# Trace of batched matrix products: six unread products per row in TensorE's last row loop

## The chip, the cores and the metric

The kernel runs on one NeuronCore of a Trainium2 chip. The metric is the time of one execution on the device in microseconds (us). A core has five engines that run their own instruction streams and meet at semaphores: TensorE (PE in the profile; its weight loads are PEld), VectorE (DVE), ScalarE (ACT), GpSimd (POOL) and SyncE (SP). Each engine has a sequencer, which carries out waits, register arithmetic and branches and hands the rest to the engine. TensorE reads two operands from the on-chip memory and writes products to PSUM. Transfers from the chip's main memory run on 16 DMA engines.

## The reference

For 8 pairs of square matrices of 2176 x 2176 in float32, the result is the trace of each product:

```python
B, N = 8, 2176

def reference(a, b):
    prod = np.matmul(a, b)
    traces = np.diagonal(prod, axis1=1, axis2=2).sum(axis=-1)
    return traces.astype(np.float32)
```

The trace of a product needs no product: it is the sum over all i and k of a[i, k] times b[k, i]. So the work is to read both matrices once (8 x 2 x 18.9 MB), transpose one, multiply element by element and add up.

## The kernel before, in words

A batch is handled in pieces of 128 partitions. A matrix has 17 strips of 128 rows; a partition holds 17 rows of 2176 elements in bfloat16 (the transfers convert). `at` holds the transposed first matrix, `rows_b` the second one (and, before that, part of the first), `a_six` the rest of the first.

For each batch TensorE transposes the first matrix block by block into three PSUM slots (`slots`, lines 345 and 348), ScalarE (line 237) and VectorE (line 266) copy the slots into `at`, and VectorE multiplies `at` by `rows_b` and reduces in one instruction (`multiply_reduce`, line 249). GpSimd issues nearly all transfers (line 169), SyncE turns landings into counts for TensorE.

The last batch is treated differently. Its second matrix arrives in ten pieces (`pieces`): rows 0 to 4, 5 to 8, 9 and 10, 11 and 12, then rows 13, 14 and 15 alone, then the last row (16) in three pieces: a long one (columns 768 to 2175), columns 256 to 767, and columns 0 to 255. Each has a semaphore in `d_late`. The seven pieces of whole rows are `whole`. VectorE takes columns 0 to 1663 of each row (`SHARE` is 1664) and of the last row columns 768 to 1663. TensorE takes the rest: the last four blocks of 128 columns of each row (`ON_TENSOR` is 4), and of the last row also columns 0 to 767. It multiplies a block of `at` by the same block of `rows_b` and adds it onto one 128 x 128 tile, `trace_ps`, whose diagonal holds the wanted sums.

TensorE's part of this is the body named "close". It runs after the transposes of the last batch:

1. It waits until the PSUM slot of the last transposes is free, and makes a matmul of a zero tile (line 309) that starts the accumulation.
2. A loop over rows 0 to 15 (line 311, `first` is a register that holds the row's first column). Each turn waits on `landed` and lowers it by one (line 312), then makes four products whose addresses are worked out from `first` (line 315). SyncE raises `landed` by a piece's number of rows when the piece is there (lines 192 to 194).
3. For the three pieces of the last row it waits on the piece's own semaphore and makes four, four and two products with fixed addresses (line 321). The last one signals `added`.

VectorE then takes the diagonal of `trace_ps` into `sums`, TensorE adds over the partitions (line 353), VectorE reduces to eight numbers (line 296) and SyncE stores them (line 357).

VectorE's own loop over the pieces of the last batch covers the pieces of whole rows and the long piece of the last row.

Of the kernel before, what the change touches and what calls it, by code (L numbers as in the profile page):

```python
# [22 lines left out]
def kernel(  # L23
# [6 lines left out]
    nc = tc.nc  # L30
    P = 128
    BATCH, N, N2 = a.shape
    assert N == N2 and N % P == 0
    NT = N // P
# [7 lines left out]
    f32 = mybir.dt.float32  # L42
    MUL, ADD = mybir.AluOpType.mult, mybir.AluOpType.add
    SLOTS = 3
    ON_TENSOR, TAKEN, CLOSE = 4, 4, 4
    SHARE = N - ON_TENSOR * P

    def sbuf(name, shape, dtype):
        return nc.alloc_sbuf_tensor(name, shape, dtype).ap()

    def psum(name, shape):
        return nc.alloc_psum_tensor(name, shape, f32).ap()

    at = sbuf("at", [P, NT, N], bf16)
    a_six = sbuf("a_six", [P, TWICE, N], bf16)
    rows_b = sbuf("rows_b", [P, NT, N], bf16)
    five, b_six = rows_b[:, 0:FIVE, :], rows_b[:, FIVE:, :]
    identity32 = sbuf("identity32", [P, P], f32)
    identity16 = sbuf("identity16", [P, P], bf16)
# [5 lines left out]
    slots = [psum(f"aT{k}", [P, 8, P]) for k in range(SLOTS)]  # L65
# [50 lines left out]
    def flat(t):  # L116
        return t.rearrange("p r k -> p (r k)")
# [10 lines left out]
    class Piece:  # L128
# [9 lines left out]
    END = NT - 1  # L138
    pieces = [
        Piece(0, 5), Piece(5, 9), Piece(9, 11), Piece(11, 13), Piece(13, 14), Piece(14, 15),  # L140
        Piece(15, 16), Piece(END, NT, 6 * P, N), Piece(END, NT, 2 * P, 6 * P), Piece(END, NT, 0, 2 * P),
    ]
    whole = [piece for piece in pieces if piece.v1 < NT]

    def counted(name):
        return Counted(nc, name)
# [18 lines left out]
    gp, act, sp, dve, pe = nc.gpsimd, nc.scalar, nc.sync, nc.vector, nc.tensor  # L165
# [16 lines left out]
    for n in range(BATCH):  # L182
# [6 lines left out]
        if n == LAST:  # L189
            sp.wait_ge(d_a12.sem, 16)  # L190
        sp.sem_inc(moved)  # L191
    for k, piece in enumerate(whole):
        sp.wait_ge(d_late[k].sem, 16)
        sp.sem_inc(landed, piece.v1 - piece.v0)

# [36 lines left out]
    with nc.Fori(0, BATCH, engines=OrderedEngineSet([act.engine])):  # L232
        act.wait_ge(clear, 1).then_inc(clear, -1)  # L233
        for k, t in enumerate(on_scalar):
            _, dst, view = tiles[t]
# [12 lines left out]
    def multiply_reduce(x, y, acc, out=None):  # L248
        return dve.tensor_tensor_reduce(  # L249
            out=x if out is None else out, in0=x, in1=y, scale=1.0, scalar=0.0,  # L250
            op0=MUL, op1=ADD, accum_out=acc,
        )
# [3 lines left out]
    with nc.Fori(  # L256
        0, dve.snap(once, min_val=1, max_val=BATCH), engines=OrderedEngineSet([dve.engine]),
        hint_back_edge=True,
    ):
        for n in range(BATCH):  # L260
            for k, t in enumerate(on_vector):
                _, dst, view = tiles[t]
                if k == 0 and n:
                    dve.wait_ge(product.sem, 2 * n).then_inc(clear, 1)
                dve.wait_ge(for_vector, len(on_vector) * n + k + 1)
                ins = dve.tensor_copy(out=dst, in_=view(slots[t % SLOTS]))  # L266
                if t != on_vector[-1]:
                    ins.then_inc(free[t % SLOTS], 1)
                else:
                    vector_done.by(ins)  # L270
            dve.wait_ge(vector_done.sem, n + 1).then_inc(free[on_vector[-1] % SLOTS], 1)
            dve.wait_ge(scalar_done.sem, n + 1).then_inc(free[on_scalar[-1] % SLOTS], 1)
            if n == LAST:
                continue
            for k, (load, t, v0) in enumerate(((d_b5, five, 0), (d_b6, b_six, FIVE))):
                dve.wait_ge(load.sem, 16 * (n + 1))
                product.by(multiply_reduce(
                    flat(at[:, v0:v0 + t.shape[1], :]), flat(t), sums[:, TAKEN * n + k:TAKEN * n + k + 1],
                ))
        taken = TAKEN * LAST  # L280
        for k, piece in enumerate(pieces[:len(whole) + 1]):
            if piece is whole[-1]:
                dve.wait_ge(parts.sem, k)
                parts.by(dve.reduce_sum(
                    out=sums[:, taken:taken + 1], in_=late[:, 0:k], axis=mybir.AxisListType.X,
                ))
            close = piece.v1 == NT
            acc = sums[:, taken + 1 + close:taken + 2 + close] if close or piece is whole[-1] else late[:, k:k + 1]
            dve.wait_ge(d_late[k].sem, 16)
            x, y = (t[:, piece.v0:piece.v1, piece.lo:N - CLOSE * P if close else SHARE] for t in (at, rows_b))  # L290
            parts.by(multiply_reduce(x, y, acc))
        dve.wait_ge(added.sem, 1)
        parts.by(multiply_reduce(identity32, trace_ps, sums[:, taken + 3:], out=diagonal))

        dve.wait_ge(summed.sem, 1)
        resulted.by(dve.reduce_sum(  # L296
            out=result[:1, :], in_=total.rearrange("o (b n) -> o b n", n=TAKEN),
            axis=mybir.AxisListType.X,
        ))


    alone = OrderedEngineSet([pe.engine])
    with nc.Fori(0, 2, engines=alone) as turn:
        fork = nc.cur_bb
        pe.br_eq(turn, 1, on_true="close", on_false="stream")
        with nc.body("close", valid_engines=alone):
            last = on_scalar[-1] % SLOTS
            pe.wait_ge(free[last], 1 + uses[last])
            pe.matmul(trace_ps, diagonal, diagonal, start=True, stop=False)
            x, y = flat(at), flat(rows_b)  # L310
            with nc.Fori(SHARE, SHARE + END * N, N, engines=alone) as first:
                pe.wait_ge(landed, 1).then_inc(landed, -1)  # L312
                for c in range(ON_TENSOR):
                    block = bass.ds(first + c * P, P)
                    pe.matmul(trace_ps, x[:, block], y[:, block], start=False, stop=False)  # L315
            for k, piece in enumerate(pieces):
                if piece.v1 == NT:
                    pe.wait_ge(d_late[k].sem, 16)
                    for c in range(N - CLOSE * P if piece.hi == N else piece.lo, piece.hi, P):
                        block = slice(END * N + c, END * N + c + P)  # L320
                        ins = pe.matmul(  # L321
                            trace_ps, x[:, block], y[:, block],
                            start=False, stop=piece.lo == 0 and c + P == piece.hi,
                        )
            added.by(ins)
            pe.br("meet")
        with nc.body("stream", valid_engines=alone):
            pe.wait_ge(ready.sem, 3)
            with nc.Fori(0, BATCH, engines=alone, hint_back_edge=True):
                for n, (moves, _, _) in enumerate(tiles):  # L330
                    use, k = divmod(n, SLOTS)
                    ps = slots[k]
                    if n == 0:
                        pe.wait_ge(moved, 1)
                    if use:
                        pe.wait_ge(free[k], 1 + use)
                    else:
                        pe.wait_ge(free[k], 1 + uses[k]).then_inc(free[k], -uses[k])  # L338
                    if n == HEAD:
                        pe.wait_ge(moved, 2)  # L340
                    elif n == NECK:
                        pe.wait_ge(moved, 3).then_inc(moved, -3)
                    for dtype, place, src in moves:
                        if dtype == f32:
                            last = pe.transpose(ps[:, place, :], src, identity32)  # L345
                        else:
                            ps16 = ps.bitcast(bf16).rearrange("q a b -> q (a b)")
                            last = pe.transpose(ps16[:, place * P:(place + 1) * P], src, identity16)  # L348
                    last.then_inc(for_vector if n in on_vector else for_scalar, 1)
            pe.br("meet")  # L350
        nc.switch_bb("meet", parent=fork)
# [39 lines left out]
```

## Time and profile before

| what | value |
|---|---|
| median of 3 runs | 705.87 us (705.86 to 705.91) |
| the profiled execution | 706.03 us |
| its span, first to last instruction | 704.6 us |
| PE, PEld busy | 204.9 us (29%), 181.4 us (26%) |
| DVE busy | 382.8 us (54%) |
| ACT busy | 207.4 us (29%) |
| POOL busy | 25.6 us (4%) |
| read from main memory over the span | 430 GB/s |
| mean granted clock of TensorE | 0.645 of full speed |

Busy shares are means over the whole span; here the last 35 us, from the moment TensorE enters "close", are what the change touches. The rows of the sequencer (marked PEldq in the views by line) give register, wait and branch instructions, with their own duration; what passes between two of them is seen only from their starts. Ends of matmuls are modelled, so the distance between starts is the better measure of their pace. The granted clock is given in shares of full speed.

### The profile page before, as it was taken

The numbers are of one execution on the slowest core, as the hardware profiler recorded it, in microseconds if no ns is written. First come the engines' busy times: TensorE is split into PE (matmuls) and PEld (weight loads), VectorE is DVE, ScalarE is ACT, GpSimd is POOL, SyncE is SP. The second block draws the span as 40 slices with busy tenths as digits, with TensorE's granted clock in tenths as the row PEclk, the third lists the DMA queues.
The fourth block names the chain that finished last, engine by engine and source line by source line (L and its number), as shares of the span: only waits on it lengthen the run. The fifth ranks groups of instructions, "written<-read, shape, count | busy, mean of one in ns | idle before, by whom it ended". The sixth has DMA issues, their size and how long they took to land. (4 is left out here: it accounts for less than half of the span.)

```text
span 704.6 us, 3799 instructions
## 1 busy us (share of the span) xinstructions
PE 204.9 (29%) x1573; PEld 181.4 (26%) x1573; DVE 382.8 (54%) x101; ACT 207.4 (29%) x162; POOL 25.6 (4%) x47
## 2 busy tenths in 40 slices
PE   0335012450124401244013440134301243014633
PEld 0334012440124401244012430134301243014522
DVE  0105487154871539716396163962639616396388
ACT  2427002370034600346003450044500455005900
POOL 1000000000000000000000000000000000001100
PEclk9759555795556855579556785557855677555955
DMA  9999999999999999999999999999999999999998
GB/s 264 218 211 208 225 217 213 217 225 213 209 227 211 215 213 229 213 213 223 215 210 213 222 221 210 230 216 210 212 226 213 213 217 226 206 219 225 212 209 172
DMA packets 7844, 152.66 MB, mean 217 GB/s; under 512 B 674, under 2 KB 930, under 8 KB 1442
## 3 DMA queue, kind: packets, MB, share of 16 engines
q0 software_dynamic: 7696, 150.41, 99.6%
q10 hardware_dynamic: 144, 2.23, 0.8%
q8 instruction: 1, 0.02, 0.0%
q14 instruction: 1, 0.01, 0.0%
q1 hardware_dynamic: 2, 0.00, 0.0%
HBM read 303.04 MB, written 0.00 MB: 430 GB/s over the span
## 5 line engine op out<-in xcount | busy, mean ns | idle before, releaser
L237 ACT COPY at<-aT 128x1536 bf16<-128x1536 bf16 (+3 forms) x160 | 202.3, 1358 | 450.6 <-ACTq L233 358.7
L249 DVE CUSTOM_DVE_ANT_0 at<-at,rows_b 128x10880 bf16<-128x10880 bf16 (+3 forms) x18 | 278.6, 15484 | 98.9 <-DMA rows_b<-in_b_dram 84.1
L266 DVE COPY at<-aT 128x1536 bf16<-128x1536 bf16 (+1 forms) x48 | 80.1, 1669 | 213.0 <-PE aT L345 161.9
L345 PE MATMUL aT<-identity,rows_b 128*128 128x128 f32 x240 | 54.6, 418 | 370.3 <-PEq L338 282.9
L345 PEld LDWEIGHTS aT<-identity,rows_b 128*128 128x128 f32 x240 | 46.7, 220 | 376.5 <-issue 283.7
L345 PE MATMUL aT<-identity,a_six 128*128 128x128 f32 x576 | 89.9, 317 | 94.1 <-SPq L191 80.3
L345 PEld LDWEIGHTS aT<-identity,a_six 128*128 128x128 f32 x576 | 82.5, 205 | 100.9 <-issue 89.1
L348 PE MATMUL aT<-identity,a_six 128*128 128x128 bf16 x480 | 34.2, 221 | 10.3 <-ACT at L237 9.2
L348 PEld LDWEIGHTS aT<-identity,a_six 128*128 128x128 bf16 x480 | 29.4, 119 | 14.7 <-ACT at L237 12.9
L169 POOL DMA_DIRECT2D rows_b<-in_b_dram x24 | 14.2, 614 | 335.0 <-PE aT L348 335.0
L249 DVE CUSTOM_DVE_ANT_1 at<-at,rows_b 128x3328 bf16<-128x3328 bf16 (+2 forms) x4 | 23.0, 5790 | 6.1 <-DMA rows_b<-in_b_dram 6.1
L315 PE MATMUL trace<-rows_b,at 128*128 x64 | 11.3, 285 | 20.5 <-PEq L312 20.5
L348 PE MATMUL aT<-identity,rows_b 128*128 128x128 bf16 x200 | 16.5, 255 | 0.4 <-DVE at L266 0.4
L348 PEld LDWEIGHTS aT<-identity,rows_b 128*128 128x128 bf16 x200 | 16.2, 132 | 0.9 <-DVE at L266 0.5
L169 POOL DMA_DIRECT2D rows_b<-in_a_dram x8 | 4.6, 577 | 293.9 <-DVE sums L249 292.0
L315 PEld LDWEIGHTS trace<-rows_b,at 128*128 x64 | 6.6, 104 | 25.1 <-issue 23.3
L231 ACT CAST rows_b<-rows_b 128x4352 bf16<-128x4352 f32 x1 | 3.8, 3817 | 8.3 <-DMA rows_b<-in_a_dram 8.3
L169 POOL DMA_DIRECT2D a_six<-in_a_dram x9 | 6.1, 678 | 0.0
L231 ACT ACT_TABLE_LOAD x1 | 1.3, 1283 | 1.9 <-PEq L175 1.9
L321 PE MATMUL trace<-rows_b,at 128*128 128x128 bf16 x10 | 1.4, 308 | 0.8 <-DMA rows_b<-in_b_dram 0.7
L249 DVE DVE_READ_ACCUMULATOR2_ANT sums<- 128x1 f32 x17 | 1.4, 83 | 0.0
L321 PEld LDWEIGHTS trace<-rows_b,at 128*128 128x128 bf16 x10 | 0.9, 135 | 1.2 <-DMA rows_b<-in_b_dram 1.2
(17 smaller groups left out, 3.3 us busy)
## 6 DMA issues: line engine op xcount, KB each, us to landing
a_six<-in_a_dram POOLq DMA_DIRECT2D x7, 6528.0 KB, 54.7
rows_b<-in_b_dram POOLq DMA_DIRECT2D x7, 6528.0 KB, 52.3
rows_b<-in_b_dram POOLq DMA_DIRECT2D x8, 2720.0 KB, 21.9
rows_b<-in_a_dram POOLq DMA_DIRECT2D x7, 2720.0 KB, 24.7
a_six<-in_a_dram POOLq DMA_DIRECT2D x2, 3264.0 KB, 47.0
rows_b<-in_a_dram ACTq DMA_DIRECT2D x1, 2176.0 KB, 10.7
rows_b<-in_b_dram POOLq DMA_DIRECT2D x1, 2176.0 KB, 31.2
rows_b<-in_b_dram POOLq DMA_DIRECT2D x2, 1088.0 KB, 38.1
```

Source lines behind the costliest of these rows:

```text
L169: count.by(gp.dma_start(out=dst, in_=src), 16)
L231: rounded.by(act.copy(out=flat(five[:, 0:FIRST, :]), in_=words))
L237: ins = act.copy(out=dst, in_=view(slots[t % SLOTS]))
L249: return dve.tensor_tensor_reduce(out=x if out is None else out, in0=x, in1=y, scale=1.0, scalar=0.0, op0=MUL, op1=ADD, accum_out=acc,)
L266: ins = dve.tensor_copy(out=dst, in_=view(slots[t % SLOTS]))
L315: pe.matmul(trace_ps, x[:, block], y[:, block], start=False, stop=False)
L321: ins = pe.matmul(trace_ps, x[:, block], y[:, block], start=False, stop=piece.lo == 0 and c + P == piece.hi,)
L345: last = pe.transpose(ps[:, place, :], src, identity32)
L348: last = pe.transpose(ps16[:, place * P:(place + 1) * P], src, identity16)
```

## The change

Three things are altered, all for the last batch.

- The row loop in "close" has 17 turns instead of 16. At the head of each turn, ahead of the wait on `landed`, stands an inner loop of three turns with two matmuls each: the 128 x 128 identity by the last 512 columns of row 0 of `at`, written to four blocks of the PSUM slot that the last transposes used. Nothing reads these products.
- The long piece of the last row, of which TensorE takes four blocks, becomes the 17th turn. It is released by SyncE through `landed`, which now loops over `shared` (the whole pieces and the long one) instead of `whole`.
- The two other pieces of the last row are done behind the loop as before, with fixed addresses. The constant `CLOSE`, which equalled `ON_TENSOR`, is gone.

```diff
-    ON_TENSOR, TAKEN, CLOSE = 4, 4, 4
+    ON_TENSOR, TAKEN = 4, 4
+    TURNS, EACH_TURN = 3, 2
...
     whole = [piece for piece in pieces if piece.v1 < NT]
+    shared = pieces[:len(whole) + 1]
...
-    for k, piece in enumerate(whole):
+    for k, piece in enumerate(shared):
         sp.wait_ge(d_late[k].sem, 16)
         sp.sem_inc(landed, piece.v1 - piece.v0)
...
-        for k, piece in enumerate(pieces[:len(whole) + 1]):
+        for k, piece in enumerate(shared):
...
-            x, y = (t[:, piece.v0:piece.v1, piece.lo:N - CLOSE * P if close else SHARE] for t in (at, rows_b))
+            x, y = (t[:, piece.v0:piece.v1, piece.lo:SHARE] for t in (at, rows_b))
...
             x, y = flat(at), flat(rows_b)
-            with nc.Fori(SHARE, SHARE + END * N, N, engines=alone) as first:
+            spare = slots[last][:, 0:ON_TENSOR, :].rearrange("q b p -> q (b p)")
+            with nc.Fori(SHARE, SHARE + END * N + 1, N, engines=alone) as first:
+                with nc.Fori(0, TURNS, engines=alone):
+                    for _ in range(EACH_TURN):
+                        pe.matmul(spare, identity16, at[:, 0, SHARE:], start=True, stop=True)
                 pe.wait_ge(landed, 1).then_inc(landed, -1)
                 for c in range(ON_TENSOR):
                     block = bass.ds(first + c * P, P)
                     pe.matmul(trace_ps, x[:, block], y[:, block], start=False, stop=False)
             for k, piece in enumerate(pieces):
-                if piece.v1 == NT:
+                if piece not in shared:
                     pe.wait_ge(d_late[k].sem, 16)
-                    for c in range(N - CLOSE * P if piece.hi == N else piece.lo, piece.hi, P):
+                    for c in range(piece.lo, piece.hi, P):
                         block = slice(END * N + c, END * N + c + P)
```

## The prediction

> **What bounds the kernel now.** I read the page first, then the chain of waits, then TensorE's timeline of the last 35 us, then the rows of TensorE's sequencer, then the clock by windows.
>
> ```profile
> span 704.6 us, 3799 instructions
> ...
> DMA  9999999999999999999999999999999999999998
> ```
>
> The transfer engines are busy in every slice, so only the stretch after the last landing can become shorter, and anything that ends before that landing costs nothing. The chain ends like this:
>
> ```profile
> 653.67 48.08 DMA rows_b<-in_b_dram
> 701.75 0.04 issue
> 701.80 0.84 PE trace L321 x6
> 702.64 0.02 issue
> 702.66 0.29 DVE diagonal L249
> 702.95 0.02 DVE sums L249
> 702.97 0.04 issue
> 703.01 0.28 PE total L353 x2
> 703.29 0.02 issue
> 703.31 0.18 DVE result L296
> ```
>
> The last bytes are there at 701.75. Six products of TensorE, two small VectorE steps, a two-part product and the store follow: 704.6 - 701.8 = 2.8 us, of which TensorE has 0.84 + 0.28. This is all that the change could shorten. The reader should next see how TensorE's row loop stands to the landings (start, length, and in brackets the idle time before):
>
> ```profile
> 668.34 0.23 PE L309 MATMUL trace<-diagonal 128*128 128x128 bf16 x1 [1.57 <-DVEq L272]
> 671.25 0.72 PE L315 MATMUL trace<-rows_b,at 128*128 x4 [2.68 <-PEq L312]
> 672.43 0.69 PE L315 MATMUL trace<-rows_b,at 128*128 x4 [0.46 <-PEq L312]
> 673.62 0.69 PE L315 MATMUL trace<-rows_b,at 128*128 x4 [0.51 <-PEq L312]
> 674.76 0.73 PE L315 MATMUL trace<-rows_b,at 128*128 x4 [0.45 <-PEq L312]
> 675.94 0.73 PE L315 MATMUL trace<-rows_b,at 128*128 x4 [0.45 <-PEq L312]
> ...
> 681.52 0.69 PE L315 MATMUL trace<-rows_b,at 128*128 x4 [4.84 <-PEq L312]
> ...
> 686.67 0.69 PE L315 MATMUL trace<-rows_b,at 128*128 x4 [0.93 <-PEq L312]
> ...
> 691.84 0.73 PE L315 MATMUL trace<-rows_b,at 128*128 x4 [3.29 <-PEq L312]
> ...
> 699.67 0.73 PE L315 MATMUL trace<-rows_b,at 128*128 x4 [1.91 <-PEq L312]
> ```
>
> Rows 0 to 4 have all landed at 671.0, so the turns at 671.25 to 675.94 run as fast as the loop can: (675.94 - 671.25)/4 = 1.17 us a turn. Waits for landings end at 681.5 (row 5), 686.7 (row 9), 691.8 (row 11) and 699.7 (row 15). The loop has slack, and the last row waits for its bytes.
>
> **How much a turn may cost.** The new loop has 17 turns. Its first unread products can be issued behind the matmul at 668.34, ahead of a wait that ends at 671.0; that is 2.6 us of cover for one turn's products, and I cost these at nothing (without the cover, one time the addition worked out below). The real products of the first turn then still start at 671.25, and those of the last turn 16 turns later, at 671.25 + 16 T. In the old loop the last turn begins at 699.67, and its closing branch is issued at 700.2 (first and last start of the branches, below) and takes 0.08, so the products behind the loop can begin about 0.70 after the first product of the last turn. They begin at 701.80 now. The loop is harmless up to 671.25 + 16 T + 0.70 = 701.80, so **T = 1.865 us**. All above that is multiplied by 16.
>
> **What one turn costs the sequencer.** The turn of 1.17 us holds only 0.7 us of products; the rest is control work of TensorE's sequencer (ns as least/median/most, then first and last start):
>
> ```profile
> L311 PEldq MOVE  x17: 29/29/38, 668.3 to 697.9; - x17
> L311 PEldq ALU_OP  x16: 36/36/36, 671.7 to 700.1; - x16
> L311 PEldq COMPARE_BRANCH  x16: 76/213/213, 671.8 to 700.2; - x16
> ...
> L312 PEldq EVENT_SEMAPHORE  x16: 51/51/51, 671.0 to 699.4; - x16
> ...
> L315 PEldq FUSED_REGOPS  x64: 51/55/60, 671.1 to 700.0; - x64
> ```
>
> A turn has one wait, four address computations, one count, one branch and one move: 51 + 4 x 55 + 36 + 213 + 29 = 549 ns in eight instructions, so about (1172 - 549)/8 = 78 ns pass between two of them. A branch that jumps back takes 213, one that falls through 76. Between count (671.7) and branch (671.8) about 0.1 us pass, of which the count itself is 36, so 60 ns is the smaller gap.
>
> The inner loop adds per row: one move to set its counter, three counts, two branches back and one that falls through. By durations that is 29 + 3 x 36 + 2 x 213 + 76 = 639 ns. With seven gaps of 60 to 78 ns it is 1.06 to 1.19 us. I take 1.15, nearer the larger gap since that one is from this very loop. **T = 1.17 + 1.15 = 2.32 us**; with no gap at all it would be 1.81.
>
> The products need no address computation, as their operands are fixed, and I cost their issue at nothing. The trace shows such pairs passing while the sequencer goes on:
>
> ```profile
> L338 PEldq EVENT_SEMAPHORE  x3: 51/51/37439, 589.9 to 627.6; - x3
> ```
>
> The first of these three waits ends at 589.9 + 37.44 = 627.3 and the third starts at 627.6; between them stand ten pairs of weight load and transpose (two tiles of five), with fixed addresses. If a pair took the sequencer 0.1 us, this would be over 1 us, and it is 0.3.
>
> **What one turn costs the array.** No product of 512 columns is in the trace; I bound it by four of 128:
>
> ```profile
> 646.65 2.56 PE L348 MATMUL aT<-identity,rows_b 128*128 128x128 bf16 x25
> ...
> 663.68 0.83 PE L348 MATMUL aT<-identity,a_six 128*128 128x128 bf16 x12
> ```
>
> At the full clock twelve take 0.83 us, with about 0.22 for the end of the last: 0.055 each. At half clock the six behind the loop take 0.84 with 0.31 for the last: 0.106. So 512 columns are 0.22 to 0.43 us, six of them 1.3 to 2.55, and with the four real products a turn needs 1.55 us (full clock) or 3.0 (half). Which one holds is read from windows of 3.41 us (busy time, count, granted clock):
>
> ```profile
> 641.92:645.34 3.42, 2.08 (x10) 0.50 1.00 214
> 645.34:648.75 3.41, 3.41 (x27) 0.50 1.14 245
> 648.75:652.16 3.41, 3.06 (x30) 1.00 1.14 245
> ...
> 655.58:658.99 3.41, 2.16 (x30) 1.00 0.81 175
> ...
> 665.82:669.23 3.41, 0.76 (x7) 1.00 0.95 204
> 669.23:672.64 3.41, 0.93 (x6) 0.50 0.82 174
> 672.64:676.06 3.42, 2.01 (x13) 0.50 1.09 234
> ```
>
> After a full window (3.41 of 3.41) the clock goes from 0.5 to 1.0; 2.16 holds it; after 0.76 it falls; 2.01 in the row loop doesn't raise it. In the changed loop the array at half clock gets 3.0 us of work per 2.32 us, so it is full from 672.1 on, the window to 676.06 is full and the clock rises there. From then on 1.55 of 2.32 us is 67% busy, more than the 63% of the window that held. What queued up in those four us is worked off in the two turns after, as the array then needs 0.8 us less than the sequencer. So the sequencer sets the pace. This needs the sequencer to run ahead of the array past a wait, which it does:
>
> ```profile
> L340 PEldq EVENT_SEMAPHORE  x1: 51/51/51, 647.4 to 647.4; - x1
> ```
>
> That wait stands behind the 25 transposes that start at 646.65 and take 2.56 us, and is passed at 647.4.
>
> **The sum.** Last turn at 671.25 + 16 x 2.32 = 708.37; products behind the loop at 709.07, that is 7.27 later than 701.80. No turn from the sixth on waits for a landing: row 5 comes up at 682.9 (landed 681.5), row 9 at 692.1 (686.7), row 15 at 706.1 (699.7). What is gained: at full clock the six products take 5 x 0.05 us less, and the short product of line 353 a little: 0.30. Span 704.6 + 7.27 - 0.30 = 711.6; the profiled execution was 706.03, 1.43 over its span and 0.16 over the median of 705.87. On the median: 705.87 + 6.97 = **712.8 us**.
>
> **The other parts cost nothing.** The long piece of the last row is released by SyncE through the counter instead of directly: one more of SyncE's 17 ns waits and a hop under 0.1 us, covered by the 7 us by which the loop is late for it (uncovered: 0.1). VectorE's share of that piece is the same expression, no transfer is added or moved, and the unread products go to a PSUM slot already released for line 309. What stands behind TensorE's late end is VectorE's diagonal step, the total, the result and the store, each late by the same 7 us.
>
> **Rivals.**
> *The control work is cheap (not slower).* The gaps of 60 to 78 ns may belong to the address computations or to recording rather than to the inner loop's counts and branches. By durations alone T = 1.81, the last turn is at 700.2 and the products behind the loop could start at 700.9, before their bytes at 701.75. Then only the clock gain is left: 705.87 - 0.30 = 705.6. It decides at T = 1.865. Against it: the gap between a count and its branch is seen, with no address in between. Chance 0.13.
>
> *Each unread pair costs the sequencer its issue.* Without the wait, count, branch and move with their gaps (329 + 4 x 60 ns), four pairs take 0.60 of the old turn, 0.15 each, 0.095 without the address computation. Six would add 0.57: T = 2.89, 705.87 + 16 x 2.89 - 30.15 = 722.0 (30.15 is 701.80 - 671.25 - 0.70 + 0.30). Against it stand the ten pairs in 0.3 us. Chance 0.09. The Trainium skill (TensorE: Matmul & The Clock Gate, section "Wait — 56ns, not 53.3ns?") states about 62 ns of sequencer microcode per matmul when hardware decoding is off; by that the estimate would be 6 x 0.062 = 0.37 us a turn and about 6 us more than my sum. The same ten pairs speak against it here.
>
> *The clock stays at half, so the change doesn't do what its products could do.* Then the array sets T = 3.0: 705.87 + 48.0 - 29.85 = 724.0. Against it: each full window in the rows above is followed by 1.0. Chance 0.07.
>
> **How the numbers follow.** Forecast 0.71, with its own range of 709.0 to 716.0 (T from 2.08, half the gaps, to 2.52, for branches that refetch slowly). The range takes in the case of paid issue, up to 722.0, which leaves 0.20 out. About 0.2% (1.4 us) is what can be told from no change; on the near side the cheap loop gives 0.11 for the same and 0.02 for faster, since only 2.8 us lie behind the last landing; slower has 0.87.
>
> **What would show it.** Right: the row loop's real products 2.2 to 2.45 us apart, no idle time put down to the wait of the row loop from row 5 on, the granted clock at 1.0 from about 676, a chain that ends in TensorE's row loop instead of a transfer, and the six products behind the loop in about 0.5 us some 7 us later. Wrong: waits for landings still seen at rows 9 to 15 (cheap control work), turns of 2.9 (paid issue), or a clock of 0.5 to the end.

## The result, and the profile after

The changed kernel takes 712.62 us (median of 6 runs, 712.34 to 713.89) against 705.89 us before (6 runs): a ratio of 1.0099, with a 95% interval of 1.0089 to 1.0109. The forecast was 712.8 us.

The chain of waits of the changed kernel no longer ends in a transfer (start, length, what):

```profile
706.65 1.46 PE aT L317 x6
708.12 0.48 PE trace L321 x4
708.60 0.04 issue
708.64 0.52 PE trace L327 x6
709.16 0.02 issue
709.18 0.29 DVE diagonal L251
```

Line 317 is the unread products, line 321 the real products of the row loop and line 327 the six behind it. The last two pieces landed within 0.1 us of where they landed before; the products behind the loop now begin at 708.64 instead of 701.80, 6.84 us later. They take 0.52 instead of 0.84. From their start to the end of the span (711.1) it is 2.46 us instead of 2.80.

TensorE's timeline of the changed kernel shows where the 6.84 us come from:

```profile
668.74 2.72 PE L317 MATMUL aT<-at,identity 128*128 128x512 bf16 x6
671.32 0.68 PE L321 MATMUL trace<-rows_b,at 128*128 x4
672.28 1.48 PE L317 MATMUL aT<-at,identity 128*128 128x512 bf16 x6 [0.28 <-issue]
673.61 0.63 PE L321 MATMUL trace<-rows_b,at 128*128 x4
674.62 1.46 PE L317 MATMUL aT<-at,identity 128*128 128x512 bf16 x6 [0.38 <-issue]
675.92 0.66 PE L321 MATMUL trace<-rows_b,at 128*128 x4
...
706.65 1.46 PE L317 MATMUL aT<-at,identity 128*128 128x512 bf16 x6 [0.34 <-issue]
707.97 0.63 PE L321 MATMUL trace<-rows_b,at 128*128 x4
```

The real products come every (707.97 - 671.32)/16 = 2.29 us, and no turn is put down to a wait for a landing. The idle time that is left, about 0.35 a turn, is put down to "issue", time in which nothing that the profile shows was waited for; the experiments below ask whether it is the sequencer's. The rows of the sequencer by line (line 315 is the inner loop):

```profile
L315 PEldq ALU_OP  x51: 36/36/36, 668.8 to 707.5; - x51
L315 PEldq COMPARE_BRANCH  x51: 76/207/208, 668.9 to 707.6; - x51
L315 PEldq MOVE  x17: 29/29/29, 668.7 to 706.6; - x17
```

There are 51 counts, 51 branches and 17 moves, three counts and branches and one move in each of 17 turns, with nearly the durations of the outer loop's.

### The profile page after: what moved, and what is told of

Read it like the earlier page. It is cut to its first block, busy times and chain, and to the rows that moved or that the text cites. A ratio compares the mean times of both kernels' runs of the same rounds, so it can differ in the third digit from the quotient of the medians.

```text
span 711.1 us, 4131 instructions
## 1 busy us (share of the span) xinstructions
PE 227.1 (32%) x1675; PEld 188.5 (27%) x1675; DVE 382.8 (54%) x101; ACT 207.4 (29%) x162; POOL 25.6 (4%) x47
## 5 line engine op out<-in xcount | busy, mean ns | idle before, releaser
L317 PE MATMUL aT<-at,identity 128*128 128x512 bf16 x102 | 26.1, 393 | 5.5 <-issue 5.5
L317 PEld LDWEIGHTS aT<-at,identity 128*128 128x128 bf16 x102 | 7.8, 98 | 17.3 <-issue 17.2
```

The source lines that it names most:

```text
L317: pe.matmul(spare, identity16, at[:, 0, SHARE:], start=True, stop=True)
```

## The experiments

Every version computes the eight traces in full; only unread products and their control are varied, or where the long piece of the last row is done. Times before are from the same chip as each run.

**The same six products without the inner loop.**

```diff
-                with nc.Fori(0, TURNS, engines=alone):
-                    for _ in range(EACH_TURN):
-                        pe.matmul(spare, identity16, at[:, 0, SHARE:], start=True, stop=True)
+                for _ in range(TURNS * EACH_TURN):
+                    pe.matmul(spare, identity16, at[:, 0, SHARE:], start=True, stop=True)
```

> The same six unread products per row, written out without the inner loop. If the sequencer's control work (counts, branches, move of the inner loop) sets the pace, a turn falls from 2.29 to about 1.55 us (the array at full clock: 6 x 0.215 + 4 x 0.056), the loop waits for landings again from row 5 on, and the time is 705.6 us: on time, less 0.3 for the faster clock behind the loop. If the products themselves set the pace, the turn stays at 2.29 and the time near 712.6. If the issue of each pair is paid for, the turn is about 1.17 + 0.57 = 1.75 and the time about 705.7 too, but the first four turns show it.

Measured: 705.86 us against 705.93, ratio 0.9998 (0.9989 to 1.0007). TensorE's timeline:

```profile
678.05 0.39 PE L320 MATMUL trace<-rows_b,at 128*128 x4
678.27 1.46 PE L316 MATMUL aT<-at,identity 128*128 128x512 bf16 x6
679.57 0.39 PE L320 MATMUL trace<-rows_b,at 128*128 x4
679.79 1.46 PE L316 MATMUL aT<-at,identity 128*128 128x512 bf16 x6
681.08 0.39 PE L320 MATMUL trace<-rows_b,at 128*128 x4
```

A turn is 1.52 us with no idle time in this stretch: the array has become the bound of the turn. The unread products are all there, and the 6.7 us are gone. So the loss comes with the inner loop and not with the products. (The turn that follows a wait is longer: row 15's products start at 700.39 and the next row's at 702.61, 2.22 us: 0.63 for row 15's products, 0.29 idle, and 1.29 from the first of the six unread ones.)

**The inner loop with products of almost nothing.** Here 16 columns take the place of 512.

```diff
-                        pe.matmul(spare, identity16, at[:, 0, SHARE:], start=True, stop=True)
+                        pe.matmul(spare[:, 0:16], identity16, at[:, 0, SHARE:SHARE + 16], start=True, stop=True)
```

> The inner loop as it is (three turns of two), but the unread products have 16 columns instead of 512. The control-work theory keeps 2.29 us a turn, with the clock at 0.5 and so without the 0.3 us gained behind the loop: 713.0 us. If the products' 512 columns set the pace, the turn falls to about 1.2 and the time to 705.9.

Measured: 712.90 us (4 runs, 712.73 to 714.16), ratio 1.0100 (1.0085 to 1.0116). The timeline has the same pace:

```profile
671.38 0.68 PE L321 MATMUL trace<-rows_b,at 128*128 x4 [1.54 <-PEq L318]
673.66 0.69 PE L321 MATMUL trace<-rows_b,at 128*128 x4 [0.28 <-PEq L318]
675.95 0.71 PE L321 MATMUL trace<-rows_b,at 128*128 x4 [0.29 <-PEq L318]
```

A turn is 2.29 us with hardly any array work. Together with the run above this separates the two: leaving out the loop and keeping the products removes the cost; keeping the loop and leaving out nearly all of the products' columns keeps it. The clock stayed at half (its mean is 0.643 here and 0.645 before), which the chain shows in the six products behind the loop:

```profile
708.77 0.81 PE trace L327 x6
```

The changed kernel has 0.52 there; the difference is the 0.3 us that the faster clock is worth when all bytes have landed.

**Twice as many thin products in the same loop** (four per inner turn instead of two).

```diff
-    TURNS, EACH_TURN = 3, 2
+    TURNS, EACH_TURN = 3, 4
```

> Three inner turns of four unread products of 16 columns (twelve per row instead of six; the loops, counts and branches are the same as in the run with two thin ones, 2.29 us a turn and 712.9 us). If the issue of a pair costs the sequencer nothing, the turn stays at 2.29 and the time at 712.9. If each pair is paid with 0.06 to 0.095 us, the turn is 2.65 to 2.86 and the time 718.7 to 722.

Measured: 712.82 us (2 runs). The turns are unchanged:

```profile
682.57 0.73 PE L321 MATMUL trace<-rows_b,at 128*128 x4 [0.23 <-PEq L318]
683.58 1.05 PE L317 MATMUL aT<-at,identity 128*128 128x16 bf16 x12 [0.28 <-issue]
684.87 0.69 PE L321 MATMUL trace<-rows_b,at 128*128 x4 [0.25 <-PEq L318]
```

From 682.57 to 684.87 it is 2.30 us with twelve pairs where it was 2.29 with six. Issuing a pair with fixed addresses costs the sequencer nothing that shows.

**Twelve products of 512 columns, written out.** The edit is that of the first run with twice the count.

> Twelve unread products per row of 512 columns, written out without inner loop. The sequencer needs 1.2 us a turn, the array 12 x 0.2155 + 4 x 0.056 = 2.81 at full clock, so the array is now the bound: 705.9 + 16 x 2.81 - 30.15 = 720.7 us, and up to 2.8 more for a first turn at half clock, which here is not made up for. If only control work counted, it would be near 705.9.

Measured: 727.66 us (2 runs), 4 to 7 us above what was expected. The timeline shows why:

```profile
666.63 0.53 PE L353 MATMUL aT<-identity,a_six 128*128 128x128 bf16 x6 [0.48 <-ACT at L239]
674.45 0.28 PE L311 MATMUL trace<-diagonal 128*128 128x128 bf16 x1 [7.29 <-issue]
674.65 4.40 PE L316 MATMUL aT<-at,identity 128*128 128x512 bf16 x12
678.89 0.39 PE L320 MATMUL trace<-rows_b,at 128*128 x4
...
681.70 0.39 PE L320 MATMUL trace<-rows_b,at 128*128 x4
...
723.90 0.39 PE L320 MATMUL trace<-rows_b,at 128*128 x4
```

The pace is as expected: (723.90 - 681.70)/15 = 2.81 us, the array's 12 x 0.2155 + 4 x 0.056. But the first matmul of "close" starts at 674.45, over 5 us later than in the other kernels (668.3 to 669.4), idle for "issue". That, and a first turn at half clock (674.65 to 678.89), is what the forecast lacked. The price of an array-bound turn is confirmed; the late start is taken up below.

**Fewer turns of the inner loop, the same products.**

```diff
-    TURNS, EACH_TURN = 3, 2
+    TURNS, EACH_TURN = 2, 3
```

> The same six unread products per row, as two turns of three. The control-work theory takes one inner turn (0.38 us) off: a turn of 1.91 us, 0.045 over the break-even of 1.865, so 16 x 0.045 - 0.3 = +0.4: 706.3 us. If the products set the pace, nothing changes: 712.6.

Measured: 706.93 us against 705.93, ratio 1.0013 (1.0004 to 1.0022): 1.0 lost instead of 0.4. The timeline:

```profile
681.44 0.65 PE L321 MATMUL trace<-rows_b,at 128*128 x4 [0.20 <-PEq L318]
683.73 0.39 PE L321 MATMUL trace<-rows_b,at 128*128 x4
685.63 0.39 PE L321 MATMUL trace<-rows_b,at 128*128 x4
...
702.75 0.39 PE L321 MATMUL trace<-rows_b,at 128*128 x4
703.03 0.50 PE L327 MATMUL trace<-rows_b,at 128*128 128x128 bf16 x6
```

A turn is (702.75 - 683.73)/10 = 1.90 us, as forecast: one inner turn less is 0.39 us. But turn 5 waited for its landing (the 0.20 of idle time), so the last turn counts from there and not from row 0, and after that wait the next row's real products came 2.29 us later, behind six unread ones that the array began only at 682.44. The products behind the loop start at 703.03, 1.23 after the old 701.80; less 0.3 for the clock this is the 1.0.

**One turn of the inner loop, the same products.** The edit sets the two constants to 1 and 6.

> The same six unread products per row, as one inner turn of six. The control-work theory takes two inner turns of 0.38 us off: 1.53 us a turn for the sequencer, 1.52 for the array at full clock. Both are under what the landings allow (1.78 us from row 5 on), so the time is 705.9 us, as without the inner loop. If the products set the pace: 712.6.

Measured: 706.65 us against 706.04, ratio 1.0007 (0.9998 to 1.0016). The last turns:

```profile
699.75 0.67 PE L321 MATMUL trace<-rows_b,at 128*128 x4
700.77 1.46 PE L317 MATMUL aT<-at,identity 128*128 128x512 bf16 x6 [0.34 <-issue]
702.06 0.39 PE L321 MATMUL trace<-rows_b,at 128*128 x4
702.28 0.50 PE L327 MATMUL trace<-rows_b,at 128*128 128x128 bf16 x6
```

Row 15's bytes land at 699.4 as before, and six unread products (1.46 us) stand between its real products and those of the long piece, 2.31 us later. That delays the products behind the loop by 0.48, most of which the faster clock makes up: the span is 704.6 us (median of 11 executions) against 704.7 before. The 0.6 us that are lost lie outside the span: the time is 1.97 us longer than the span in the median, and 1.33 before; what that is the profile doesn't show.

**The moved piece alone**, without inner loop and unread products.

```diff
-                with nc.Fori(0, TURNS, engines=alone):
-                    for _ in range(EACH_TURN):
-                        pe.matmul(spare, identity16, at[:, 0, SHARE:], start=True, stop=True)
```

> The long piece as the 17th turn of the row loop, without inner loop and without unread products. If moving the piece costs nothing, the turns are 1.17 us, the clock 0.5 and the time 705.9 us as before. A rival in which the way over SyncE's count or the 17th turn is late gives up to 706.6.

Measured: 706.15 us against 705.93, ratio 1.0002 (0.9993 to 1.0011): by the medians 0.2 us, which the interval doesn't tell from nothing. The profiled execution took 706.80 us, the longest of the 11. In it the piece of 512 columns, for which the products behind the loop wait first, landed at 702.3, and the end of the chain reads:

```profile
702.01 0.69 PE trace L318 x4
702.70 0.80 PE trace L324 x6
```

Where the kernel before started the last six products 0.05 us after that landing, here they start 0.4 after it, behind the long piece's turn with its wait, address computations and branch. From the landing of the very last piece (256 columns) to VectorE's diagonal step it is 0.88 us (702.65 to 703.53) instead of 0.61 (702.05 to 702.66), so the move costs about 0.3.

**The long piece kept apart**, in the kernel before: 16 turns, six unread products written out.

```diff
+            spare = slots[last][:, 0:ON_TENSOR, :].rearrange("q b p -> q (b p)")
             with nc.Fori(SHARE, SHARE + END * N, N, engines=alone) as first:
+                for _ in range(6):
+                    pe.matmul(spare, identity16, at[:, 0, SHARE:], start=True, stop=True)
                 pe.wait_ge(landed, 1).then_inc(landed, -1)
```

> Six unread products per row written out without an inner loop, in a row loop of 16 turns; the long piece of the last row stays behind the loop with its own wait and fixed addresses, as in the kernel before. If the move of the long piece costs about 0.25 us behind the last landing (0.2 more than the kernel before in the run without products) and the faster clock gains 0.3 to 0.35, this gives 705.6 us, 0.25 below the version with the piece moved. If the move costs nothing, it is the same as that one, 705.85.

Measured: 708.42 us against 706.04, ratio 1.0036 (1.0023 to 1.0050). The row loop was on time; the chain shows a gap inside the total:

```profile
702.63 0.21 PE total L356
702.84 2.58 issue
705.42 0.22 PE total L356
```

The two halves of one product stand 2.58 us apart, and no semaphore that the profile shows was waited for. But something was transferred in that time. The list of DMA queues for 702.84 to 705.42 has one row (packets, MB, share of 16 engines):

```profile
q8 instruction: 1, 0.02, 2.7%
```

It is a block of 16 KB on an instruction queue, moved from 702.87 to 703.99 (2.7% of 2.58 us on 16 engines is 1.1 us of one engine). Three more runs asked where this comes from. Two have three and four unread products per row:

> As the run with the long piece kept apart and six unread products written out (708.42 us), but three per row. In that run all products ended in time and the two halves of the last product (the total) stood 2.6 us apart, idle for nothing that the profile shows. If that gap comes from where the instructions lie, six instructions fewer move it away and the time is 705.6 us: the bytes of the last piece as before, less 0.3 for the faster clock. If the gap comes from the unread products or the faster clock, it stays: about 708.4.

> The same with four unread products per row. By the place of the instructions: no gap, or one of another size at another place (705.6 us without one); by the products or the clock: 708.4.

Measured: 706.18 us (ratio 1.0004, 0.9995 to 1.0013) and 706.58 us (1.0008, 0.9999 to 1.0017) against 705.90. The gap is gone in both, and no gain is left either. With four the span is 704.5 us, 0.1 below the kernel before, and the loss lies outside the span (2.09 us in the median instead of 1.33; 1.59 with three), as in the run with one inner turn. The third keeps the six and puts eight thin ones ahead of the loop:

```diff
+            for _ in range(8):
+                pe.matmul(spare[:, 0:16], identity16, at[:, 0, SHARE:SHARE + 16], start=True, stop=True)
             with nc.Fori(SHARE, SHARE + END * N, N, engines=alone) as first:
```

> The run with the long piece kept apart and six unread products written out (708.42 us), and ahead of its row loop, once, eight more unread products of 16 columns: 16 instructions that shift all that follows them, while the loop itself is the same. They run behind the first wait for a landing, 1 us of work in 2.5. If the gap of 2.6 us in the total comes from where its instructions lie, it goes away, or shows at another place or size: 705.6 to 706.6 us when gone. If it comes from the six products per row or the clock they hold, it stays: 708.4.

Measured: 706.51 us against 705.90, ratio 1.0009 (1.0000 to 1.0018). The chain:

```profile
702.49 0.65 PE trace L326 x6
...
703.51 0.23 PE total L358 x2
```

The total's halves are together again. The work of the loop is that of the run with the gap; 16 instructions more lie ahead of the total. So the gap doesn't come from six products per row or the clock they hold, and most likely from where its instructions lie. That the sequencer was short of instructions is the likely cause, of this gap and of the late start with twelve products. In the idle time of that one (667.16 to 674.45) such a block moved too, from 671.50 to 672.45:

```profile
q8 instruction: 1, 0.02, 0.8%
```

There the sequencer's count of the outer loop stands at 666.9 and its branch at 673.9. The cause is still argued: the profile doesn't say for which engine the block is, work goes on only 1.4 to 2 us after it has come, and in the other runs such a block moves and no unexplained gap of TensorE goes with it. The 0.6 us by which the shifted run lies above the kernel before are in the landings: the piece of 512 columns is there at 702.44 instead of 701.75.

**The changed kernel once more**, for its spread.

> The changed kernel once more, for its spread: two of six runs stood at 713.89 us, the others at 712.34 to 712.73. If the pace of the loop alone sets the time, most runs lie near 712.6; the runs 1.4 us higher should come again in about one of three, and a profile that falls among them should show a later first turn or a gap that the loop doesn't explain.

Measured: 712.49 us (4 runs: 712.37, 712.43, 712.56 and 713.74). The higher runs come again, one in four; the profile fell among the others, with 2.29 us a turn as before. Such shifts are in the traces of other runs. In 12 of the 14 the first landing of the last batch is taken up by SyncE at 670.7 to 671.7; without the inner loop and with three products per row kept apart it is 672.3, about 1.3 us later. Row 15 lands at 699.1 to 699.6 in nine traces and about 0.7 later, at 700.0 to 700.1, in five. In just these five an instruction block of 16 KB moved while the matrices were still arriving (the two with the late first landing at 670.2, the run without products at 671.4, the one with twelve at 671.5, the shifted one at 51.2); in the nine others it moved behind the last landing. So the delay goes with the block; that the block causes it is not shown. A loop that runs at its own pace from the first landing on would show a first landing 1.3 us late in full. The higher runs have no profile, so that this is their cause is not shown.

## Why the prediction was right

**The pace of the loop.** Forecast 2.32 us, measured 2.29. The inner loop's control work was forecast at 1.06 to 1.19 and taken as 1.15; it is 2.29 - 1.17 = 1.12. The two runs that exchange loop and products against each other show that it is this work, and the run with one inner turn less gives 0.39 us for a count and a branch back with their gaps (36 + 213 + two gaps of 60 to 78, that is 0.37 to 0.41).

**The sum.** Last turn forecast at 708.37, measured 707.97; products behind the loop 709.07 against 708.64; gain by the clock 0.30 against 0.34; span 711.6 against 711.1; time 712.8 against 712.62. Sixteen times the 0.03 us by which the turn was too long is 0.5, about the whole difference of the spans. That the times agree to 0.2 is in part luck: the profiled execution lay 0.16 above its median before and 0.11 below it after, which hides 0.27.

**Free issue.** Shown, by twelve pairs of 16 columns in the same turn as six.

**The clock.** It rose, but one window earlier than forecast. Windows of 3.41 us of the changed kernel (busy time, count, granted clock):

```profile
665.19:668.60 3.41, 1.36 (x19) 1.00 1.10 236
668.60:672.02 3.42, 3.37 (x11) 0.50 1.00 214
672.02:675.43 3.41, 2.77 (x14) 1.00 0.98 209
```

The first six unread products, 2.72 us at half clock, with the zero tile's product ahead of them and the first four real ones behind, filled the window that ends at 672.02. I had them as covered and did not count what they do to the clock. It changed nothing, as the sequencer sets the pace at either clock in the first turns.

**What was wrong: the point from which a turn is late.** The prediction counted only from the first landing and had T = 1.865. Every later landing sets a bound of its own, and the last one is the tightest: row 15's products start at 699.67, one turn follows, and 699.67 + T + 0.70 must not pass 701.80, so T = 1.43. Even that is too generous, as a turn behind a wait is longer than the pace of the loop: 2.29, 2.31 and 2.22 us in the runs with two inner turns, one and none, with paces of 1.90, 1.52 and 1.52. None of this had a part in the forecast, as a turn of 2.3 is late from every landing; but the rival of cheap control work, with T = 1.81, would have been late by about 0.4 us at the last row and not have given 705.6. The run with turns of 1.90 us shows it, with 1.0 us above the kernel before. In the run with one inner turn the products behind the loop were late by 0.48, but the 0.6 us of its time are outside the span and no sign of it.

**What was read wrongly: the last bytes.** Not all are there at 701.75, as the prediction has it. That is the landing of the piece of 512 columns; the last one, of 256, is issued at 654.20 and takes 47.9 us, so it is there at about 702.05. The changed kernel is late for both, so the forecast didn't suffer. A version that is on time has its last two products wait for that piece, and the faster clock gains less than the prediction's 0.30 there: from this landing to VectorE's diagonal step it is 0.61 us before and 0.36 with four products kept apart.

**What was too cheap: the moved piece.** Uncovered it was costed at 0.1 us. The trace without products shows about 0.3, and the medians 0.2. In the changed kernel it is covered. It is also about what the faster clock gains, which is the likely reason why the version without the inner loop comes out at no change.

**The rivals.** Paid issue and a clock at half are out. No version was faster than the kernel before beyond what can be measured: the 2.8 us behind the last landing leave little to win, and each version gave the gain of the clock back: to the moved piece, to the unread products in the last turn, to the gap, to later landings, or to time outside the span that stays open.

## What to carry to other kernels

Cost a loop by its control instructions before its work: on TensorE a turn of a small loop cost about 0.39 us here whether it held two products of 512 columns or of 16, and a written-out body of the same products was free up to the array's own time. Filler that holds a clock must fit between each landing and the end, not only between the first landing and the end; the turn behind the last wait is the one to check, as it took 2.2 to 2.3 us here where the others took 1.5 to 1.9. What was hidden behind waits for transfers comes out multiplied by the number of turns as soon as the loop no longer waits.

## What the runs showed of the hardware that was not expected

- A product's two halves stood 2.58 us apart, and in another kernel the first matmul behind a branch came over 5 us late, both without a semaphore to wait for; an instruction block of 16 KB moved in each of the two gaps, and a shift by 16 instructions took the first away.
- In the five traces where such a block moved before the last landing, row 15 landed about 0.7 us later than in the nine others (700.0 to 700.1 instead of 699.1 to 699.6).
- At half clock the first six products of 512 columns, with five of 128, filled a window and the clock rose at its end (668.60 to 672.02, 3.37 of 3.42 us busy). In the kernel before, 2.01 us of 3.42 did not raise it.
- A row's four real products, whose addresses are worked out from a register, ran at 0.056 us each behind unread ones (four within 0.39 us, of which 0.22 is the end of the last) where the sequencer was ahead of the array, and at 0.14 where it was behind (0.63).
